# B's queries and scores ahead of A's in a hybrid-attention layer, with query and key copies made on chip

## The chip, the cores and the metric

The kernel runs on one core of a Trainium2 chip. The metric is the device time of one execution in microseconds (us), the median of several runs on the same chip.

## The reference

Two decoder layers run for a prompt of 1024 tokens and 32 sample tokens (8 sequences of 4). Layer 0 is the one that the change touches:

```python
qa, ka, va, qb, kb, vb, z = split(x @ w_in)       # rotary on qa, ka, qb, kb
oa = banded_attention(qa, ka, va, 128, sinks)     # A: 8 query heads, 2 key heads of 64
for g, (window, dil) in enumerate([(128, 1), (512, 4), (2048, 16)]):
    obs[g], lses[g] = banded_attention(to_sub(qb[g], dil), to_sub(kb[g], dil),
                                       to_sub(vb[g], dil), window // dil)
ob = sum(softmax(lses)[g] * obs[g])               # B: three dilated groups, merged
mix = concat([oa, ob]) * silu(z)
x = layer_norm(ALPHA * x + mix @ w_out)
```

The sample tokens do the same against caches. Layer 1 is an mLSTM (chunkwise matrix memory) with its own projections and out-projection. All of it is in float32.

## The kernel before

Every product of float32 matrices is made from pairs of fp32r tiles: a high part (rounded copy, `hi`, on ScalarE) and a low part (the difference, `lo`, on VectorE), three matmuls for one (L199 to L201 for projections, tile `pj`).

Layer 0 first projects keys and values (`proj_kv`, to about 110 us). Then 24 feature tiles of 128 columns follow, 72 matmuls each: 16 for the queries (`proj_q(g)`, g = 0 is A, g = 1, 2, 3 are B with dilation 1, 4, 16, four tiles each), 8 for the gates (`proj_z0(j)`; for j < 4 it also loads A's finished output, `ao`, and its reciprocal denominators, `aF`, and multiplies them in). Queries go as high and low rows to a DRAM tensor `QQ[g]` and are read back by head.

Attention runs by group g, key head kv (0 or 1) and quarter hf of the tokens. First a statistics pass: scores `st` from the high parts alone (L437, queries in `QZ`), their masked row maximum on VectorE (L441, `ST`), transposed (`trm`) and written negated (`NM`) into row 128 of QQ. For B the three groups share one maximum: each group's row goes through `NMB` and `nr` (`attn_b_max`). Then come the scores `sc`: L466 multiplies K1 (high keys twice) with Q1 (low and high queries), L467 K2 (low keys and a row of ones) with Q2 (high queries and the row of negative maxima). ScalarE takes the exponential (L469), GpSimd masks it (L472 to L480), `hi` and `lo` split it (`ph`, `pl`; every fourth `pl` of B on GpSimd), and three matmuls `av` (L489 to L491) multiply it with V. A block is 2 `sc` and 3 `av`. VectorE adds `av` into `OD` (L535, L582, L584). At a half's end `OD` is stored to DRAM, and `finish` loads the denominators back (`dn`), inverts them and stores them (`FD`). All these DMAs are issued by SP, whose queue runs in order: a wait at one holds those behind it.

`weave` takes steps of several generators in proportion to given weights, which sets the order in which code is written; attention is written with a higher scheduling priority (`ahead`), and a scheduler then decides the order on each engine. The first weave puts A's attention and the statistics of B's groups 1 and 2 next to `proj_q(1..3)`; the second puts the statistics of group 3, B's attention for kv = 0 and 9 steps of kv = 1 next to the gates. What is left of kv = 1 runs with the sample attention (`sS`, `so`, tiles `KT`) and the merges, and the out-projection (`py`, weights `wo` split into `oh` and `ol`) follows.

Of the kernel before, what the change touches and what calls it, by code (L numbers as in the profile page):

```python
# [61 lines left out]

AHEAD = (1000, 1000, 60, 300)

W1, W2, W3, W4 = (129, 76), (86, 80), (28, 15, 6), (64, 90)

EARLY = 9

# [29 lines left out]
class Builder:  # L98
# [118 lines left out]
    def proj_q(self, g):  # L217
        nc = self.nc
        dil = DIL[g]
        QQ = self.QQ[g]  # L220
        for j in range(4):
            sh = self.stage.tile([128, T], F32R, tag="sh", name="sh")
            sl = self.stage.tile([128, T], F32R, tag="sl", name="sl")
            qs = self.stage.tile([128, TS], F32, tag="qs", name="qs")

            def evac(c, t0, n, ps):
                src = ps
                if j == 3:
# [12 lines left out]

                s = src[:, :n]
                if dil > 1:
                    s = s.rearrange("p (n r) -> p n r", r=dil)
                self.hi(pv(sh), s, 0.125)
                self.lo(pv(sl), s, pv(sh), 0.125)

            yield from self.proj_feat(self.A['w0f'][4 + 4 * g + j], self.X0, evac)
            r0 = 128 * ((j + 1) % 4)
            self.store('q', QQ[512 + r0:640 + r0, :], f(sh[:, :TP]))  # L250
            self.store('q', QQ[r0:r0 + 128, :], f(sl[:, :TP]))
            self.store('q', self.QS[g, r0:r0 + 128, :], qs)

    def proj_kv(self):
        nc, A, O = self.nc, self.A, self.O
        tc = self.tc
        with tc.tile_pool(name="kvp", bufs=1) as kp, tc.tile_pool(name="kvt", bufs=2) as kt:
# [36 lines left out]
            for j in range(4):  # L294
                sh = self.stage.tile([128, T], F32R, tag="sh", name="sh")
                sl = self.stage.tile([128, T], F32R, tag="sl", name="sl")
                self.hi(sh[:, :TP], KF[:, j, :TP])
                self.lo(sl[:, :TP], KF[:, j, :TP], sh[:, :TP])
                r0 = 128 * ((j + 1) % 4)
                for u in range(2):  # L300
                    self.store('k', self.KK[512 * u + r0:512 * u + r0 + 128, :], f(sh[:, :TP]))
                self.store('k', self.KK[1024 + r0:1152 + r0, :], f(sl[:, :TP]))
                self.store('k', self.KS[r0:r0 + 128, :], KF[:, j, TP:T])
            wv = []
            for k in range(0, 8, 2):
# [51 lines left out]
    def qh_load(self, g, kv, hf):  # L357

        Q = self.QZ[hf % 2]
        t = slice(256 * hf, 256 * hf + 256)  # L360
        h = slice(4 * kv, 4 * kv + 4)
        self.store("Qh", f(Q[0:64]), self.QQ[g].rearrange("(d h) t -> d h t", h=8)[64:128, h, t])
        return Q

    def q2_load(self, g, kv, hf):
        Q2 = self.qp.tile([65, 4, 256], F32R, tag="Q2", name="Q2")
        t = slice(256 * hf, 256 * hf + 256)
        h = slice(4 * kv, 4 * kv + 4)
        self.load(f(Q2), self.QQ[g].rearrange("(d h) t -> d h t", h=8)[64:129, h, t])
        return Q2  # L370

    def k1_load(self, g, kv):
        nc = self.nc
        dil = DIL[g]
        src = self.KK.rearrange("(d h) t -> h d t", h=8)[2 * g + kv][0:128]
        K1 = self.kp.tile([128, TP], F32R, tag="K1", name="K1")
        if dil == 1:
            self.load(f(K1), src)
        else:
            kt = self.kp.tile([128, TP], F32, tag="kt", name="kt", bufs=1)  # L380
            self.load(kt, src)
            nc.vector.tensor_copy(K1.rearrange("p (r n) -> p n r", r=dil), kt.rearrange("p (n r) -> p n r", r=dil))
        return K1

    def k2_load(self, g, kv):
        nc = self.nc
        dil = DIL[g]
        src = self.KK.rearrange("(d h) t -> h d t", h=8)[2 * g + kv][128:192]
        K2 = self.kp.tile([65, TP], F32R, tag="K2", name="K2")
        if dil == 1:  # L390
            self.load(f(K2[0:64]), src)
        else:
            kt = self.kp.tile([128, TP], F32, tag="kt", name="kt", bufs=1)
            self.load(kt[0:64], src)
            nc.vector.tensor_copy(K2[0:64].rearrange("p (r n) -> p n r", r=dil),
                                  kt[0:64].rearrange("p (n r) -> p n r", r=dil))
        nc.gpsimd.memset(f(K2[64:65]), 1.0)
        return K2

    def v_load(self, g, kv):  # L400

# [119 lines left out]

    def attn_a(self, kv):
        nc = self.nc
        K1, K2, V = self.k1_load(0, kv), self.k2_load(0, kv), self.v_load(0, kv)
        ST = self.sm.tile([128, 32], F32, tag="ST", name="ST")
        for hf in range(4):
            Q1 = self.qh_load(0, kv, hf)
            yield from self.stats(0, kv, hf, Q1, K1, ST)
        nc.vector.tensor_tensor(ST, ST, self.sinkb[:, 32 * kv:32 * kv + 32], OP.max)
        nm = self.QQ[0][1024 + 4 * kv:1028 + 4 * kv]  # L530
        self.neg_rows(ST, nm)
        OD = self.odp.tile([65, 4, TP], F32, tag="OD", name="OD")

        def emit(qb, av):
            nc.vector.tensor_copy(self.od_view(OD, 0, qb), self.av_view(av[0:65], 0))  # L535

        for hf in range(4):
            Q1 = self.q1_load(0, kv, hf)
            Q2 = self.q2_load(0, kv, hf)
            yield from self.scores(0, kv, hf, Q1, Q2, K1, K2, V, emit)  # L540
        self.store('o', self.OD[0][kv], OD)
        self.finish(0, kv, nm)

    def attn_b_stats(self, g, kv):
        K1 = self.k1_load(g, kv)
# [24 lines left out]
    def attn_b(self, kv, done=None):  # L570
# [1 line left out]
        nc = self.nc  # L572
        OD = self.odp.tile([65, 4, TP], F32, tag="OD", name="OD")
        for g in (3, 2, 1):
            K1, K2, V = self.k1_load(g, kv), self.k2_load(g, kv), self.v_load(g, kv)

            def emit(qb, av, g=g):
                o = self.od_view(OD, g, qb)
                a = self.av_view(av[0:65], g)
                if g == 3:  # L580
                    for s in range(2):
                        nc.vector.tensor_copy(o[:, :, s, :], a[:, :, s, :])  # L582
                else:
                    nc.vector.tensor_tensor(o, a, o, OP.add)  # L584
                if g == 1 and qb in (2, 5, 7):
                    t = slice(CH[qb // 3][0], 128 * qb + 128)
                    self.store('o', self.OD[1][kv][:, :, t], OD[:, :, t])
                    if done:
                        done(qb // 3)

            for hf in range(4):
                Q1 = self.q1_load(g, kv, hf)
                Q2 = self.q2_load(g, kv, hf)
# [295 lines left out]
    def layer0(self):  # L889
# [4 lines left out]
        self.QQ = [dt(f"QQ{g}", [129 * 8, TP]) for g in range(4)]  # L894
        self.QS = dt("QS", [4, 512, TS])

        self.KK, self.KS = dt("KK", [3 * 512, TP]), dt("KSd", [512, TS])
# [16 lines left out]
        with tc.tile_pool(name="qp", bufs=2) as self.qp, tc.tile_pool(name="kp", bufs=2) as self.kp, \  # L914
# [9 lines left out]
            self.QZ = [sm.tile([128, 4, 256], F32R, name=f"QZ{u}") for u in range(2)]  # L924
            for Q in self.QZ:
                nc.gpsimd.memset(f(Q[64:128]), 0.0)
            run(self.proj_q(0))
            self.done = 0
            self.bps = AB_PS[0]

            def projections():
# [1 line left out]
                    yield from self.proj_q(g)  # L933
                    self.done = g

            def attention():
                for kv in range(2):
                    yield from self.attn_a(kv)
                for g in (1, 2):
                    while self.done < g:  # L940
                        yield None
                    for kv in range(2):
                        yield from self.attn_b_stats(g, kv)

            weave((projections(), W1[0]), (ahead(tc, attention(), AHEAD[0]), W1[1]))

            tmp.release()
            tmp = self.tmp = tc.alloc_tile_pool(name="tmpz", bufs=1, side="right")

            def gate_path():  # L950
                for j in range(8):
                    yield from self.proj_z0(j)

            def last(c):
# [3 lines left out]
            def attention_b():  # L958
# [2 lines left out]
                    self.attn_b_max(kv)  # L961
                self.bps = AB_PS[1]
                yield from self.attn_b(0)
                late = self.late = self.attn_b(1, last)
                for _ in range(EARLY):
                    yield next(late)

            weave((gate_path(), W2[0]), (ahead(tc, attention_b(), AHEAD[1]), W2[1]))
            tmp.release()
# [653 lines left out]
```

## Time and profile before

| | |
|---|---|
| median of 3 runs | 1516.51 us (1511.09 to 1520.24) |
| profiled execution | 1514.5 us, span 1512.8 us |
| mean granted TensorE clock | 0.971 of full speed |
| PE / VectorE / ScalarE / GpSimd busy | 93% / 59% / 31% / 18% |
| bytes moved by DMA queues | 241.01 MB |

The span runs from the first to the last instruction. PE is TensorE's matmuls, SPq SyncE's issue queue. Line numbers are those of the kernel before.

### The profile page before, as it was taken

How to read it: one execution, taken by the hardware profiler on the slowest of the kernel's cores; microseconds unless marked ns; L12 is line 12 of the kernel's file. 1: busy time of each engine (PE TensorE's matmuls, PEld its weight loads, DVE VectorE, ACT ScalarE, POOL GpSimd, SP SyncE). 2: the span in 40 equal slices, each digit the busy share in tenths (PEclk: the TensorE clock that was granted, in tenths of full speed). 3: DMA queues.
4: the chain of work that ended last, by engine and by line, in shares of the span. 5: the costliest groups of instructions: out<-in, count | busy, mean ns of one | idle time of the engine just before them, and what ended most of it. 6: DMA issues, size and time to landing. Idle time of an engine off the chain costs nothing.

```text
span 1512.8 us, 21927 instructions
## 1 busy us (share of the span) xinstructions
PE 1409.6 (93%) x7792; PEld 1193.2 (79%) x7792; DVE 897.7 (59%) x2479; ACT 472.9 (31%) x892; POOL 276.4 (18%) x351
## 2 busy tenths in 40 slices
PE   8999999999988777978999999999999999999997
PEld 7989998998887434456879878988898899877785
DVE  5311556677655856758774536555565566566786
ACT  5331143521112654512124313331333133323310
POOL 1002252512334874401000000000000000000010
PEclk9999999999999978989999999999999999999999
DMA  8646665667747998894312565364224312341731
GB/s 304 222 150 209 212 187 184 188 199 202 205 135 183 226 228 179 260 273 137 128 51 72 193 222 178 97 217 135 70 78 124 116 49 68 118 127 28 239 133 46
DMA packets 149323, 241.01 MB, mean 159 GB/s; under 512 B 17632, under 2 KB 115904, under 8 KB 148696
## 3 DMA queue, kind: packets, MB, share of 16 engines
q1 hardware_dynamic: 141150, 218.24, 49.0%
q10 hardware_dynamic: 8064, 21.37, 3.9%
q8 instruction: 62, 1.02, 0.3%
q14 instruction: 47, 0.39, 0.1%
HBM read 178.66 MB, written 83.97 MB: 174 GB/s over the span
## 4 chain that ended last, share of the span: by engine, by line
PE 67%; DMA 18%; DVE 7%; issue 3%; ACT 1%; POOL 1%; SPq 1%; DVEq 0%; POOLq 0%; ACTq 0%
PE pj L199 10%; PE pj L200 10%; PE pj L201 10%; PE py L167 3%; PE py L165 3%; PE py L166 3%; PE pvo L165 3%; PE pvo L166 3%; PE pvo L167 3%; DMA G<-GR 2%; DMA Q<-QQ 2%; DMA NMB<-NM 1%; DMA QZ<-QQ 1%; DMA OD<-OD 1%; PE av L489 1%
## 5 line engine op out<-in xcount | busy, mean ns | idle before, releaser
L199 PE MATMUL pj<-x1h,wh 128*128 128x384 f32 (+1 forms) x576 | 189.7, 329 | 1.7 <-ACT QT L1156 1.6
L199 PE MATMUL pj<-xh,wh 128*128 128x384 f32 (+1 forms) x576 | 187.9, 326 | 1.2 <-DVE rt L214 1.2
L201 PE MATMUL pj<-x1h,wl 128*128 128x384 f32 (+1 forms) x576 | 187.8, 326 | 0.0
L201 PE MATMUL pj<-xh,wl 128*128 128x384 f32 (+1 forms) x576 | 187.6, 326 | 0.0
L200 PE MATMUL pj<-xl,wh 128*128 128x384 f32 (+1 forms) x576 | 187.6, 326 | 0.0
L200 PE MATMUL pj<-x1l,wh 128*128 128x384 f32 (+1 forms) x576 | 187.6, 326 | 0.0
L199 PEld LDWEIGHTS pj<-x1h,wh 128*128 128x128 f32 x576 | 108.7, 189 | 6.5 <-issue 3.3
L201 PEld LDWEIGHTS pj<-x1h,wl 128*128 128x128 f32 x576 | 108.6, 188 | 6.0 <-issue 5.8
L199 PEld LDWEIGHTS pj<-xh,wh 128*128 128x128 f32 x576 | 109.8, 191 | 4.4 <-DVE rt L214 2.2
L200 PEld LDWEIGHTS pj<-x1l,wh 128*128 128x128 f32 x576 | 108.6, 189 | 4.0 <-issue 3.8
L201 PEld LDWEIGHTS pj<-xh,wl 128*128 128x128 f32 x576 | 110.0, 191 | 1.4
L200 PEld LDWEIGHTS pj<-xl,wh 128*128 128x128 f32 x576 | 109.6, 190 | 1.1
L441 DVE CUSTOM_DVE_ANT_0 junk<-st,maskq 128x256 f32<-128x256 f32 (+1 forms) x256 | 93.0, 363 | 25.0 <-PE st L437 5.9
L165 PE MATMUL pvo<-voh,x1h 128*128 128x512 f32 x256 | 101.7, 400 | 2.5 <-DVE SZ L1172 2.5
L166 PE MATMUL pvo<-voh,x1l 128*128 128x512 f32 x256 | 100.8, 396 | 0.0
L167 PE MATMUL pvo<-vol,x1h 128*128 128x512 f32 x256 | 100.3, 395 | 0.0
L811 POOL TENSOR_TENSOR rsw<-rsw,mhalf 128x1 f32<-128x1 f32 (+1 forms) x54 | 40.2, 745 | 321.4 <-DVE rsw L810 305.6
L122 POOL TENSOR_TENSOR wl<-wr,wh 128x1024 fp32r<-128x1024 f32 x24 | 59.2, 2470 | 122.5 <-ACT qs L233 77.8
L116 DVE TENSOR_TENSOR pl<-p,ph 128x512 fp32r<-128x512 f32 x82 | 68.3, 842 | 21.7 <-ACT ph L112 15.8
L112 ACT ACTIVATE wh<-wr 128x1024 fp32r<-128x1024 f32 x48 | 50.7, 1057 | 81.5 <-PE pj L200 75.2
L112 ACT ACTIVATE ph<-p 128x512 fp32r<-128x512 f32 x100 | 61.4, 629 | 41.6 <-PE av L490 26.2
L469 ACT ACTIVATE p<-sc 128x512 f32<-128x512 f32 x100 | 56.8, 593 | 44.6 <-PE sc L467 29.1
(349 smaller groups left out, 3145.3 us busy)
## 6 DMA issues: line engine op xcount, KB each, us to landing
Q<-QQ SPq DMA_DIRECT2D x32, 512.0 KB
out_kvs_dram<-in_cache_b_kv_dram SPq DMA_DIRECT2D x16, 1022.0 KB
wr<-in_w0f_dram SPq DMA_DIRECT2D x24, 512.0 KB
wr<-in_w1f_dram SPq DMA_DIRECT2D x24, 512.0 KB
Q<-QQ SPq DMA_DIRECT2D x32, 260.0 KB
QQ<-sh ACTq DMA_DIRECT2D x16, 512.0 KB
QQ<-sl ACTq DMA_DIRECT2D x16, 512.0 KB
QZ<-QQ SPq DMA_DIRECT2D x32, 256.0 KB
```

The costliest lines, as they stand in the source:

```text
L112: return self.nc.scalar.activation(out, in_, AF.Copy, scale=scale)
L116: return self.nc.vector.tensor_tensor(out, in_, f(hi), OP.subtract)
L122: self.nc.gpsimd.tensor_tensor(out, in_, f(hi), OP.subtract)
L165: nc.tensor.matmul(ps, xh[:, k, t], wh, start=k == 0, stop=False)
L166: nc.tensor.matmul(ps, xl[:, k, t], wh, start=False, stop=False)
L167: nc.tensor.matmul(ps, xh[:, k, t], wl, start=False, stop=k == 7)
L199: nc.tensor.matmul(ps[:, :n], wh[:, k, :], xh[:, k, :n], start=k == 0, stop=False)
L200: nc.tensor.matmul(ps[:, :n], wh[:, k, :], xl[:, k, :n], start=False, stop=False)
L201: nc.tensor.matmul(ps[:, :n], wl[:, k, :], xh[:, k, :n], start=False, stop=k == 7)
L441: nc.vector.tensor_tensor_reduce(junk[:, :n], st[:, u, c0:c0 + n], mk, 1.0, -3e38, OP.add, OP.max, ST[:, 8 * h + qb:8 * h + qb + 1])
L469: nc.scalar.activation(p, sc, AF.Exp)
L811: nc.gpsimd.tensor_tensor(r, v, self.mhalf[:m], OP.pow)
```

## The change

Three edits. First, the order: A's queries are projected after B's, at the head of the second weave; A's attention moves out of the first weave into the second, behind B's attention for kv = 0; the gates come in the order 4, 5, 6, 7, 0, 1, 2, 3, and those with j < 4 wait, while code is written, until A's half is `attended`. Second, the high query rows of Q2 are copied on ScalarE from Q1, and only row 128 is loaded; QQ's high and low rows change places for it. Third, keys are stored once less, K1's second half is copied on ScalarE, and one load of 128 rows serves K1 and K2.

```diff
-W1, W2, W3, W4 = (129, 76), (86, 80), (28, 15, 6), (64, 90)
+W1, W2, W3, W4 = (129, 15), (129, 96), (28, 15, 6), (64, 90)
...
-            self.store('q', QQ[512 + r0:640 + r0, :], f(sh[:, :TP]))
-            self.store('q', QQ[r0:r0 + 128, :], f(sl[:, :TP]))
+            self.store('q', QQ[r0:r0 + 128, :], f(sh[:, :TP]))
+            self.store('q', QQ[512 + r0:640 + r0, :], f(sl[:, :TP]))
...
-                for u in range(2):
-                    self.store('k', self.KK[512 * u + r0:512 * u + r0 + 128, :], f(sh[:, :TP]))
-                self.store('k', self.KK[1024 + r0:1152 + r0, :], f(sl[:, :TP]))
+                self.store('k', self.KK[r0:r0 + 128, :], f(sh[:, :TP]))
+                self.store('k', self.KK[512 + r0:640 + r0, :], f(sl[:, :TP]))
...
-        self.load(f(Q2), self.QQ[g].rearrange("(d h) t -> d h t", h=8)[64:129, h, t])
+        self.load(f(Q2[64:65]), self.QQ[g].rearrange("(d h) t -> d h t", h=8)[128:129, h, t])
+        self.nc.scalar.activation(Q2[0:64], f(Q1[0:64]), AF.Copy)
         return Q2
...
+    def k_load(self, g, kv, low=True):
...
+            n = 128 if low else 64
             kt = self.kp.tile([128, TP], F32, tag="kt", name="kt", bufs=1)
+            self.load(kt[:n], src[:n])
+            for u, d in enumerate((K1[0:64], K2[0:64]) if low else (K1[0:64],)):
+                nc.vector.tensor_copy(d.rearrange("p (r n) -> p n r", r=dil),
+                                      kt[64 * u:64 * u + 64].rearrange("p (n r) -> p n r", r=dil))
+        nc.scalar.activation(K1[64:128], f(K1[0:64]), AF.Copy)
...
-            run(self.proj_q(0))
-            self.done = 0
+            self.done = self.attended = 0
...
-            def attention():
-                for kv in range(2):
-                    yield from self.attn_a(kv)
+            def statistics():
...
-            weave((projections(), W1[0]), (ahead(tc, attention(), AHEAD[0]), W1[1]))
+            weave((projections(), W1[0]), (ahead(tc, statistics(), AHEAD[0]), W1[1]))
...
             def gate_path():
-                for j in range(8):
+
+                yield from self.proj_q(0)
+                self.done = 4
...
+                for j in (4, 5, 6, 7, 0, 1, 2, 3):
+                    while j < 4 and self.attended <= j // 2:
+                        yield None
                     yield from self.proj_z0(j)
...
                 yield from self.attn_b(0)
+                self.bps = AB_PS[0]
+                while self.done < 4:
+                    yield None
+                for kv in range(2):
+                    yield from self.attn_a(kv)
+                    self.attended = kv + 1
+                self.bps = AB_PS[1]
```

**Where rows move.** TensorE's order where A passes from key head 0 to 1. Before, the transposition `trm` of the second half's maxima stands among projections:

```order
L200 MATMUL pj<-xl_103,wh 128x384
L201 MATMUL pj<-xh_102,wl 128x384
L199 MATMUL pj<-xh_104,wh 128x288
L466 MATMUL sc<-Q_2261,K_2056 128x512
L200 MATMUL pj<-xl_105,wh 128x288
L449 MATMUL trm<-ident,ST 32x128
L201 MATMUL pj<-xh_104,wl 128x288
L199 MATMUL pj<-xh_104,wh 128x288
```

After, at the same place (`st` are the statistics, the numbers mark tiles):

```order
L485 MATMUL av<-ph,V 66x512
L486 MATMUL av<-ph,V 64x512
L487 MATMUL av<-pl,V 66x512
L433 MATMUL st<-K_4718,QZ_951 128x256 x4
L433 MATMUL st<-K_4718,QZ_950 128x256 x8
L433 MATMUL st<-K_4718,QZ_951 128x256 x8
L462 MATMUL sc<-Q_4925,K_4718 128x512 x2
L445 MATMUL trm<-ident,ST 32x128
L463 MATMUL sc<-Q_4927,K_4719 128x512 x2
L462 MATMUL sc<-Q_4925,K_4718 128x512
L463 MATMUL sc<-Q_4927,K_4719 128x512
```

No projection row stands in the 78 rows around this place (the last one ahead of them is followed by 13 blocks of A); the next comes eight rows further on.

SyncE's DMA order at the same hand-over (OD_89 is A's output of key head 0, QQ_75 A's queries). Before:

```order
L109 DMA OD_89<-OD 65x4096
L109 DMA QZ_954<-QQ_76 64x4x256
L109 DMA wr<-in_w0f_dram 128x1024
L109 DMA dn<-OD_89 32x128
L109 DMA QZ_955<-QQ_76 64x4x256
L109 DMA QQ_75<-NM 32x128
L109 DMA FD_93<-dn 32x128
L106 DMA Q_2263<-QQ_75 65x4x256
```

And after:

```order
L109 DMA OD_89<-OD 65x4096
L106 DMA V<-VV 64x8x128
L109 DMA dn<-OD_89 32x128
L109 DMA ao<-OD_89 64x1024 x2
L109 DMA FD_93<-dn 32x128
L109 DMA aF<-FD_93 64x512 x4
L109 DMA QQ_75<-NM 32x128
L106 DMA Q_4927<-QQ_75 1x4x256
```

The row of maxima has moved behind FD and four `aF` loads, and Q2's load shrinks from 65 rows to one. TensorE's order at the end of layer 0's attention, before:

```order
L491 MATMUL av<-pl,V 66x512
L727 MATMUL so<-scrh,scrl 128x128
L165 MATMUL py<-oh,mh_5699 128x512
L166 MATMUL py<-oh,ml_5700 128x512
L165 MATMUL py<-oh,mh_5699 128x512
L166 MATMUL py<-oh,ml_5700 128x512
L165 MATMUL py<-oh,mh_5699 128x512
L166 MATMUL py<-oh,ml_5700 128x512
L732 MATMUL so<-KT,scrh 32x128 x16
```

After:

```order
L681 MATMUL sS<-KT,scrh 32x128 x8
L650 MATMUL sNew<-scrh 128x32 x4
L650 MATMUL sNew<-scrh,scrl 128x32 x4
L487 MATMUL av<-pl,V 66x512
L165 MATMUL py<-oh,mh_5725 128x512
L166 MATMUL py<-oh,ml_5726 128x512
L165 MATMUL py<-oh,mh_5725 128x512
L166 MATMUL py<-oh,ml_5726 128x512
```

Before, all sample scores `sS` stand ahead of the last `av`; after, the first eight do, and the rest with every `pT` and `so` stands behind it.

## Rows read from the trace of the kernel before

**Rows 1.** The page's head and its part 1: busy time, share, instructions.

```profile
span 1512.8 us, 21927 instructions
PE 1409.6 (93%) x7792; PEld 1193.2 (79%) x7792; DVE 897.7 (59%) x2479; ACT 472.9 (31%) x892; POOL 276.4 (18%) x351
```

**Rows 2.** Windows by stage: length, engines' busy time, granted clock, DMA share, GB/s.

```profile
110.00:320.00 210.00, 207.00 (x1233) 194.97 (x1232) 108.59 (x283) 73.88 (x134) 72.58 (x59) 0.99 0.61 191
320.00:497.00 177.00, 155.69 (x929) 146.50 (x927) 116.53 (x420) 33.36 (x62) 54.35 (x49) 0.96 0.68 191
497.00:641.00 144.00, 113.27 (x449) 59.31 (x448) 101.00 (x165) 79.66 (x155) 87.86 (x104) 0.86 0.92 224
641.00:697.00 56.00, 40.07 (x248) 28.41 (x248) 35.44 (x41) 12.86 (x16) 1.82 (x1) 0.88 0.81 237
697.00:785.00 88.00, 87.75 (x432) 70.30 (x431) 68.67 (x156) 13.19 (x25) 9.67 (x11) 1.00 0.32 104
```

**Rows 3.** Windows of 20 to 60 us inside those stages, same columns.

```profile
120.00:140.00 20.00, 20.00 (x127) 20.00 (x126) 2.66 (x5) 3.39 (x7) 6.62 (x4) 1.00 0.55 192
200.00:220.00 20.00, 20.00 (x112) 17.98 (x112) 14.70 (x22) 12.02 (x22) 12.95 (x12) 1.00 0.68 192
440.00:500.00 60.00, 49.13 (x259) 42.16 (x258) 36.49 (x99) 15.59 (x30) 22.39 (x30) 0.94 0.62 166
500.00:540.00 40.00, 31.62 (x116) 18.15 (x114) 35.92 (x47) 27.76 (x49) 38.18 (x35) 0.91 1.05 241
540.00:580.00 40.00, 25.24 (x64) 13.32 (x65) 17.37 (x29) 15.28 (x28) 19.88 (x37) 0.70 0.92 189
```

**Rows 4.** One window, instructions of projection tile pj alone (PE, PEld, DVE, ACT).

```profile
200.00:220.00 20.00, 14.42 (x81) 13.40 (x81) 3.92 (x8) 0.86 (x1) 1.00 0.68 192
```

**Rows 5.** The stage 497 to 641, tile sc alone, then av alone.

```profile
497.00:641.00 144.00, 42.04 (x114) 22.79 (x114) 35.21 (x61) 0.86 0.92 224
497.00:641.00 144.00, 65.80 (x199) 28.75 (x198) 40.84 (x58) 0.86 0.92 224
```

**Rows 6.** SyncE's timeline: start, length of issue, instruction.

```profile
262.55 0.32 SPq L109 DMA_DIRECT2D QQ<-NM  x1
...
263.96 0.78 SPq L106 DMA_DIRECT2D Q<-QQ  x2
...
318.41 0.53 SPq L109 DMA_DIRECT2D OD<-OD  x1
...
328.14 0.32 SPq L109 DMA_DIRECT2D dn<-OD  x1
...
336.32 0.32 SPq L109 DMA_DIRECT2D FD<-dn  x1
...
370.38 1.09 SPq L109 DMA_DIRECT2D aF<-FD  x2
...
375.70 1.08 SPq L109 DMA_DIRECT2D aF<-FD  x2
...
562.91 0.33 SPq L109 DMA_DIRECT2D dn<-OD  x1
...
576.66 0.32 SPq L109 DMA_DIRECT2D FD<-dn  x1
```

**Rows 7.** The page's part 6, DMA issues of Q2: count, KB each.

```profile
Q<-QQ SPq DMA_DIRECT2D x32, 260.0 KB
```

**Rows 8.** The page's part 5, groups: busy, mean ns of one, idle before.

```profile
L112 ACT ACTIVATE wh<-wr 128x1024 fp32r<-128x1024 f32 x48 | 50.7, 1057 | 81.5 <-PE pj L200 75.2
L469 ACT ACTIVATE p<-sc 128x512 f32<-128x512 f32 x100 | 56.8, 593 | 44.6 <-PE sc L467 29.1
```

**Rows 9.** PE's waits from 497 to 641: us in total, times, longest.

```profile
PE sc L467 <- DMA Q<-QQ: 7.4, 7, 3.4
PE sc L466 <- DMA Q<-QQ: 6.6, 4, 2.9
```

**Rows 10.** The stage 697 to 785, out-projection tile py alone.

```profile
697.00:785.00 88.00, 73.89 (x311) 55.10 (x309) 10.71 (x16) 1.00 0.32 104
```

More of the change, by code (lines that the diff above doesn't have):

```diff
@@ L361, in qh_load, with q2_load @@
         h = slice(4 * kv, 4 * kv + 4)
-        self.store("Qh", f(Q[0:64]), self.QQ[g].rearrange("(d h) t -> d h t", h=8)[64:128, h, t])
+        self.store("Qh", f(Q[0:64]), self.QQ[g].rearrange("(d h) t -> d h t", h=8)[0:64, h, t])
         return Q
-    def q2_load(self, g, kv, hf):
+    def q2_load(self, g, kv, hf, Q1):
         Q2 = self.qp.tile([65, 4, 256], F32R, tag="Q2", name="Q2")
@@ L368, in q2_load @@
         h = slice(4 * kv, 4 * kv + 4)
-        self.load(f(Q2), self.QQ[g].rearrange("(d h) t -> d h t", h=8)[64:129, h, t])
+        self.load(f(Q2[64:65]), self.QQ[g].rearrange("(d h) t -> d h t", h=8)[128:129, h, t])
+        self.nc.scalar.activation(Q2[0:64], f(Q1[0:64]), AF.Copy)
         return Q2
-    def k1_load(self, g, kv):
+    def k_load(self, g, kv, low=True):
         nc = self.nc
         dil = DIL[g]
-        src = self.KK.rearrange("(d h) t -> h d t", h=8)[2 * g + kv][0:128]
+        src = self.KK.rearrange("(d h) t -> h d t", h=8)[2 * g + kv]
         K1 = self.kp.tile([128, TP], F32R, tag="K1", name="K1")
+        K2 = self.kp.tile([65, TP], F32R, tag="K2", name="K2") if low else None
         if dil == 1:
-            self.load(f(K1), src)
+            self.load(f(K1[0:64]), src[0:64])
+            if low:
+                self.load(f(K2[0:64]), src[64:128])
         else:
+            n = 128 if low else 64
             kt = self.kp.tile([128, TP], F32, tag="kt", name="kt", bufs=1)
[L381 to L398, printed above, removed]
+            self.load(kt[:n], src[:n])
[3 more added lines that the diff above has]
+        nc.scalar.activation(K1[64:128], f(K1[0:64]), AF.Copy)
+        if low:
+            nc.gpsimd.memset(f(K2[64:65]), 1.0)
+        return K1, K2
     def v_load(self, g, kv):
@@ L523, in attn_a @@
         nc = self.nc
-        K1, K2, V = self.k1_load(0, kv), self.k2_load(0, kv), self.v_load(0, kv)
+        (K1, K2), V = self.k_load(0, kv), self.v_load(0, kv)
         ST = self.sm.tile([128, 32], F32, tag="ST", name="ST")
@@ L538, in attn_a @@
             Q1 = self.q1_load(0, kv, hf)
-            Q2 = self.q2_load(0, kv, hf)
+            Q2 = self.q2_load(0, kv, hf, Q1)
             yield from self.scores(0, kv, hf, Q1, Q2, K1, K2, V, emit)
@@ L544, in attn_b_stats @@
     def attn_b_stats(self, g, kv):
-        K1 = self.k1_load(g, kv)
+        K1 = self.k_load(g, kv, False)[0]
         ST = self.sm.tile([128, 32], F32, tag="ST", name="ST")
@@ L574, in attn_b @@
         for g in (3, 2, 1):
-            K1, K2, V = self.k1_load(g, kv), self.k2_load(g, kv), self.v_load(g, kv)
+            (K1, K2), V = self.k_load(g, kv), self.v_load(g, kv)
             def emit(qb, av, g=g):
@@ L592, in attn_b @@
                 Q1 = self.q1_load(g, kv, hf)
-                Q2 = self.q2_load(g, kv, hf)
+                Q2 = self.q2_load(g, kv, hf, Q1)
                 yield from self.scores(g, kv, hf, Q1, Q2, K1, K2, V, emit)
@@ L895, in layer0 @@
         self.QS = dt("QS", [4, 512, TS])
-        self.KK, self.KS = dt("KK", [3 * 512, TP]), dt("KSd", [512, TS])
+        self.KK, self.KS = dt("KK", [2 * 512, TP]), dt("KSd", [512, TS])
         self.VV = dt("VV", [TP, 8 * 128])
@@ L943, in attention @@
                         yield from self.attn_b_stats(g, kv)
-            weave((projections(), W1[0]), (ahead(tc, attention(), AHEAD[0]), W1[1]))
-            tmp.release()
-            tmp = self.tmp = tc.alloc_tile_pool(name="tmpz", bufs=1, side="right")
+            weave((projections(), W1[0]), (ahead(tc, statistics(), AHEAD[0]), W1[1]))
             def gate_path():
-                for j in range(8):
+                yield from self.proj_q(0)
+                self.done = 4
+                self.tmp.release()
+                self.tmp = tc.alloc_tile_pool(name="tmpz", bufs=1, side="right")
+                for j in (4, 5, 6, 7, 0, 1, 2, 3):
+                    while j < 4 and self.attended <= j // 2:
+                        yield None
                     yield from self.proj_z0(j)
@@ L968, in layer0 @@
             weave((gate_path(), W2[0]), (ahead(tc, attention_b(), AHEAD[1]), W2[1]))
-            tmp.release()
+            self.tmp.release()
             stage.release()
```

## The prediction

> **What bounds the kernel now.** I read the page's totals first, then the table by stage, then finer windows, then who waits for whom. TensorE (PE) is busy 1409.6 of 1512.8 us [rows 1], so time can come only from stretches where it is not full, or runs slowly. The table by stage [rows 2] shows them. From 110 to 320 us PE is busy 207.0 of 210; from 320 to 497, the end of layer 0's last projection, 155.7 of 177. From 497 to 641, B's attention with no projection left to put between its matmuls, 113.3 of 144 at a mean granted clock of 0.86. From 641 to 697 the sample attention ends and the out-projection waits for its weights and merged inputs: 40.1 of 56. From 697 to 785 the out-projection runs full. Everything behind 785 us is layer 1, which the diff does not touch. So I price three stretches: W, the 24 feature tiles (110 to 497, 387 us); U, attention without cover (144 us); T, sample and out-projection (56 + 88 = 144 us).
>
> An attention matmul has two prices. Covered: 127 projection matmuls fill 20 us, 0.157 each [rows 3]; in 200 to 220 us 112 ran without a gap, 81 of them projections [rows 3, 4], so the other 31 took 20 - 81 x 0.157 = 7.3 us, 0.23 each. Uncovered: 116 in 40 us from 500 to 540, 0.34 each, with VectorE busy 35.9 and GpSimd 38.2 of those 40 [rows 3]: the softmax engines and the loads set the pace there. A lower bound is PE's own busy time in that window, 31.6 / 116 = 0.27.
>
> **Part 1: work moved from U into W.** U holds 114 score (sc) and 199 output (av) records [rows 5]. In the order of before, 114 sc and 204 av rows stand behind the last projection; in the order after, 70 and 123, and W holds 125 more sc and av than before. Nearly all of the sample attention has left U as well: it stands behind the last av now. W pays 125 x 0.23 = **+29 us** (bounds 125 x 0.16 = 20, as if they cost what a projection does, and 125 x 0.34 = 43). U keeps 193 matmuls: 193 x 0.34 = 66 us (bounds 52 by 0.27, 66). To it comes the end of A's second half: finish() stores OD, loads dn, divides and stores FD through SP's queue, and VectorE's queue stops at dn. Before, the same end of B's first half fell into 540 to 580 us, where PE was busy 25.2 of 40 at a clock of 0.70 [rows 3], 15 us lost; with half the query bytes in the queues I take 6 (bounds 0 and 15). So U is 72 us in place of 144: **-72 us** (52 to 81).
>
> **Part 2: a new gap at A's hand-over.** Gates j < 4 are written out only once A's half is attended, so the projections run out: the order shows A's last blocks of half 0, all statistics of half 1, and the first scores of half 1 without a projection row between. About 13 blocks of 5 matmuls lose their cover; A has no GpSimd subtraction, so I charge 4 of the 65 x (0.34 - 0.23) = 7 us: **+4 us** (0 to 7). Then PE's queue holds L463's score, which needs Q2's row of negative maxima. On SP the store QQ<-NM now stands behind dn, two ao, FD and four aF; before, directly behind dn and ahead of FD. The links, from the trace: OD store to dn load 318.41 to 328.14, 9.7 us; dn to FD 8.2; FD's landing before aF may issue, taken as a 16 KB store to the next load that needs it, 262.55 to 263.96, 1.4; the second aF pair behind GpSimd's product of the first, 370.38 to 375.70, 5.3; its issues 1.1; QQ<-NM 1.4; the 4 KB row itself at most another 1.4 or so [rows 6]. That is 28.5 us. PE has 20 statistics (5 us at 0.23) and some 6 av (2 us at 0.34) in it: 21.5, **+22 us**. Bounds: if aF's wait vanishes, 22 - 5.3 = 16; with the dn to FD of the crowded 562.91 to 576.66, 13.75 [rows 6], 27. Queued behind that score are the gates' projections, so nothing fills it. The Trainium skill ("DMA: Bandwidth & Descriptors", Anatomy of one DMA) puts the fixed cost of a DMA at about 2.0 us and says that DMA engines do not wait on semaphores, the issuing sequencer does. By its cost six small links and 2.4 us of data would be 14 us, 20 with 6 of engine work, and the gap some 13, the net -14, 1500 us; the rows show 9.7 for the first link alone, and I keep the rows. Its second sentence is what the order of SP's rows makes visible: everything behind aF waits with it.
>
> **Part 3: chains that gain cover.** From 440 to 500 us, where the last B statistics, the common maximum and B's first loads follow each other, PE is busy 49.1 of 60 [rows 3]. After, the same chain has A's queries and gates 4 to 7 beside it, and I take back nearly all of the 10.9: **-10 us** (0 to -11). A's own statistics lie in such cover too, as before.
>
> **Part 4: copies in place of loads.** 32 Q2 loads of 260 KB become rows of 4 KB [rows 7], 8.2 MB; four K stores of 512 KB go, 2 MB; keys' loads lose about 3.6 MB. In exchange ScalarE makes 46 copies of 1024 elements, at 1.06 us [rows 8] 49 us on an engine that is busy 31% [rows 1]. In W it is free; in U some 12 copies come to exponentials (0.59 each [rows 8]) and splits. PE waited for Q 14.0 us in U [rows 9], which is in the 0.34 price; since the copies take back what the loads give, I leave that price. In W the queues' share is 0.61 to 0.68 [rows 2], so fewer bytes change little: **0**; what it may be worth is in the relief below.
>
> **Part 5: the tail T grows.** The sample's 16 large key and value loads now stand on SP behind the last query, between merges and weights, and 336 of the 432 out-projection matmuls behind the sample. Counted from the order behind OD's last store: 21.3 MB against 12.5. At T's 237 GB/s [rows 2] the 8.8 MB more are 37 us if transfers are the bound; the queues' share was 0.81 [rows 2], so 0 if all falls into their gaps and PE's. I take 15. Then 336 matmuls at 88 us / 311 [rows 10] are 95 for 88: +7. **+22 us** (7 to 44).
>
> **Sum.** -72 + 29 + 4 + 22 - 10 + 22 = -5. From the profiled execution's 1514.5 us this is 1509.5; the median of the runs shown is 1516.5, 0.1% above it, and I say **1509 us**. No change and 0.5% (7.6 us) can't be told apart here.
>
> **Rivals.**
> *The tail decides (slower).* At a tail of +40, near its upper bound, the net is +13: 1527 us. It decides as soon as the tail costs more than 27, where the net turns positive. For it: the sample's buffers are four deep, and SP waited for sS, which frees them, in U; a slow round in T has no attention beside it. Against it: PE is idle for 16 of those 56 us already [rows 2].
> *Copies block exponentials (slower).* ScalarE takes its queue in order; a Q2 copy at the head waits for Q1's load, and the exponentials of blocks already scored wait behind it. At 1.4 us [rows 6] for each of the 12 in U, net +12: 1527 us; it decides from 0.4 us each. Against it: two query buffers are loaded ahead.
> *The relief is worth more (faster).* If U runs at PE's own 0.27 with no gap (52 us, 20 less), and the tail costs only its 7 (15 less), net -40: 1474 us. For it: the queues' share is 1.05 from 500 to 540 [rows 3], and PE's largest waits in U are for Q [rows 9]. Against: VectorE and GpSimd are as full there.
> *Only moved (no change).* The matmuls are the same ones; if W and T give back what U saves, the time stays. In the sum 29 + 4 + 22 - 10 + 22 = 67 of the 72 do so already, so this lies inside the forecast's own spread.
>
> **How the numbers follow.** Forecast as summed, 1495 to 1523: 0.45 (0.21 faster, 0.19 same, 0.05 slower). Tail: 0.25 (0.06 same, 0.19 slower). Copies: 0.08, slower. Relief: 0.22, faster. Together faster 0.43, same 0.25, slower 0.32. The range must reach the relief's 1474 and the slower rivals' 1527, and some of each side's spread; 1473 to 1535 leaves about 2 in 10 out: the better half of the relief, both slower rivals at once, or a gap at the hand-over twice as long.
>
> **What would show it.** Right: about 70 us between the last projection and the last av; one PE gap of about 22 us some 60 us ahead of the last projection, which ends with a load of 4 KB behind QQ<-NM; out-projection starting in earnest about 70 us after the last av; layer 1 as long as before. Wrong: projections inside the hand-over, so that no gap shows; waits of exponentials for Q2's copies; or a U of over 85 us.

## The result and the profile after

The change made the kernel slower, by 1 to 1.5%: 1534.43 us median (1530.03 to 1537.07) against 1517.68 before, ratio 1.0114 (95% interval 1.0073 to 1.0156). A second measurement gave 1532.50 against 1512.06, ratio 1.0148 (1.0123 to 1.0174). The forecast was 1509, 0.5% faster.

The windows of the changed kernel, by stage, columns as in [rows 2]. The cuts are those of after: 341 is about the end of the first weave, 478 to 526 the hand-over inside A, 551 the last projection of layer 0, 634 the last av, 709 the last sample matmul, 798 the last of the out-projection.

```profile
110.00:320.00 210.00, 198.12 (x1238) 194.36 (x1237) 110.97 (x406) 53.26 (x88) 45.88 (x27) 0.98 0.56 177
320.00:341.00 21.00, 17.95 (x104) 17.15 (x103) 17.84 (x62) 3.06 (x4) 6.48 (x4) 0.93 0.39 127
341.00:478.00 137.00, 132.09 (x723) 115.20 (x722) 84.19 (x175) 79.36 (x134) 65.36 (x81) 1.00 0.51 153
478.00:526.00 48.00, 25.84 (x83) 14.78 (x82) 28.14 (x84) 16.06 (x29) 11.82 (x14) 0.68 0.45 129
526.00:551.00 25.00, 24.88 (x139) 21.31 (x138) 13.11 (x20) 14.42 (x25) 11.91 (x13) 1.00 0.30 94
551.00:634.00 83.00, 62.04 (x227) 35.51 (x225) 53.12 (x76) 54.29 (x88) 61.99 (x72) 0.84 0.60 175
634.00:709.00 75.00, 56.45 (x339) 34.98 (x338) 49.13 (x78) 21.38 (x42) 3.66 (x2) 0.76 0.96 295
709.00:798.00 89.00, 82.92 (x386) 65.71 (x382) 65.77 (x146) 11.96 (x22) 9.13 (x10) 0.94 0.33 112
```

The reader is to see three things. U, without cover, fell from about 146 us to 83. W grew from 385 to 441 (110 to 551): its one deep hole is the hand-over, PE busy 25.8 of 48 at a clock of 0.68, and it has also lost 9 us of PE between 110 and 320, where [rows 2] were full. T grew: 164 us from the last av to the last out-projection matmul, where 134.7 were needed before. The table has the last starts from the traces (projection, av, out-projection, us) and what follows from them:

| | last pj | last av | last py | W | U | T |
|---|---|---|---|---|---|---|
| before | 494.7 | 640.2 | 774.9 | | 145.5 | 134.7 |
| after | 550.9 | 633.8 | 797.9 | +56 | -63 | +29 |

Layer 1 took as long as before (736 us from the last py to the end, against 738). So the +23 us at the end of layer 0 are the whole loss.

The sample's first key loads tell where T starts. The loads of `KT` by SyncE, before and then after (median issue time, first and last start):

```profile
L106 SPq DMA_DIRECT2D KT<-in_kt_dram x12: 328/336/424, 578.2 to 617.3; - x12
```

```profile
L106 SPq DMA_DIRECT2D KT<-in_kt_dram x12: 328/368/839, 618.0 to 669.8; - x12
```

Before, the first came 62 us ahead of the last av; after, 16 us. The sample then ended 75 us behind the last av, where it had ended 21 us behind.

The hand-over, in the timelines of after, SyncE, then TensorE, then VectorE, then ScalarE (start, length, instruction, idle time and what ended it):

```profile
495.12 0.57 SPq L109 DMA_DIRECT2D OD<-OD  x1
...
503.60 0.33 SPq L109 DMA_DIRECT2D dn<-OD  x1
...
506.92 0.31 SPq L109 DMA_DIRECT2D FD<-dn  x1
508.86 6.02 SPq L109 DMA_DIRECT2D aF<-FD  x4
514.97 0.53 SPq L109 DMA_DIRECT2D QQ<-NM  x1
517.68 1.26 SPq L106 DMA_DIRECT2D Q<-QQ  x2
```

```profile
501.07 0.79 PE L433 MATMUL st<-K,QZ 128*128 128x256 f32 x2 [0.25 <-DVE ST L437]
507.23 0.79 PE L433 MATMUL st<-K,QZ 128*128 128x256 f32 x2 [5.37 <-DVE ST L437]
...
512.35 0.41 PE L445 MATMUL trm<-ident,ST 128*32 128x128 f32 x1
519.59 1.22 PE L463 MATMUL sc<-Q,K 65*128 65x512 f32 x2 [6.82 <-DMA Q<-QQ]
```

```profile
505.40 0.28 DVE L514 TENSOR_TENSOR dn<-dn,nmc 32x128 f32<-32x128 f32 x1 [4.39 <-DMA dn<-OD]
```

```profile
512.80 0.27 ACT L447 ACTIVATE NM<-trm 32x128 fp32r<-32x128 f32 x1 [22.44 <-PE trm L445]
```

The maxima were there only at 513.1 us. SyncE issued their store at 514.97, so the four aF loads ahead of it cost 2 us. What came late was the maxima themselves: VectorE stood 4.4 us at dn with statistics behind it in its queue, and PE waited 5.4 us there.

### The profile page after: what moved, and what is told of

It reads as the page before. It is cut to its first block, busy times and chain, and to the rows that moved or that the text cites. A ratio compares the mean times of both kernels' runs of the same rounds, so it can differ in the third digit from the quotient of the medians.

```text
span 1534.1 us, 22001 instructions
## 1 busy us (share of the span) xinstructions
PE 1414.5 (92%) x7792; PEld 1200.1 (78%) x7792; DVE 897.3 (58%) x2480; ACT 515.4 (34%) x938; POOL 266.6 (17%) x350
## 4 chain that ended last, share of the span: by engine, by line
PE 69%; DMA 16%; DVE 7%; issue 3%; ACT 2%; POOL 1%; SPq 1%; ACTq 0%; DVEq 0%; POOLq 0%
PE pj L199 11%; PE pj L200 10%; PE pj L201 10%; PE py L165 3%; PE py L167 3%; PE py L166 3%; PE pvo L165 3%; PE pvo L166 3%; PE pvo L167 3%; DMA wr<-in_wo_dram 3%; DMA G<-GR 2%; PE st L433 2%; DMA out_cmems_dram<-Cs 1%; DMA aF<-FD 1%; PE sc L462 1%
## 5 line engine op out<-in xcount | busy, mean ns | idle before, releaser
L116 DVE TENSOR_TENSOR pl<-p,ph 128x512 fp32r<-128x512 f32 x83 | 64.7, 794 | 42.9 <-ACT ph L112 42.1
L165 PE MATMUL py<-oh,mh 128*128 128x512 f32 x128 | 55.3, 432 | 16.0 <-ACT oh L112 10.4
L433 PE MATMUL st<-K,QZ 128*128 128x256 f32 x256 | 52.3, 299 | 18.5 <-DVE ST L437 9.6
```

The lines of the kernel that those rows point to most:

```text
L116: return self.nc.vector.tensor_tensor(out, in_, f(hi), OP.subtract)
L165: nc.tensor.matmul(ps, xh[:, k, t], wh, start=k == 0, stop=False)
L433: nc.tensor.matmul(st[:, u, :], Q1[:, h, q0:q0 + 128], K1[:, w0:w0 + 256], start=True, stop=True)
```

## The experiments

Times are medians; the ratio, with its 95% interval, is to before, measured beside it on the same chip. Where two runs of different rounds are subtracted, the medians are from different chips; by the ratios such differences come out within about 3 us of those given. W, U and T are read from the traces as above, KT is the first load of the sample's keys.

### The two halves of the change

e1 takes the copies and leaves the order of before; e2 the other way round (the diff is the one at the top, cut in two).

> The order of before, with only the copies in place of loads (QQ's rows swapped, Q2 and K1 copied on ScalarE, 14 MB fewer). If the copies are harmless, as the prediction charged them, the time is that of before within 8 us, a few us less if PE's 14 us of waits for Q in the uncovered stretch shrink: 1508 to 1518. If they block exponentials at the head of ScalarE's queue, 10 or more us above before, 1527 and up, and they carry the loss.

> The order of after, with before's loads of Q2 and keys. If the order carries the loss, this stands 15 to 30 us above before (1532 to 1547), as far as after or further, since the 14 MB come back. If the copies carry it, it falls to before or below, 1505 to 1520.

e1: 1500.40 us, 0.9930 (0.9904 to 0.9956), faster. e2: 1539.22, 1.0175 (1.0137 to 1.0212), slower. They about add up to the change: -11 and +27 make 16, where it measured 17 and 20. The order carries the loss. The copies gained more than either theory had it: U fell from 145.5 to 138.3 us and T from 134.7 to 124.8. In e1's stretch without cover, 492 to 630 us, PE's waits for Q, where [rows 9] had 14.0 us, and for ScalarE are these (us, times, longest):

```profile
PE av L485 <- ACT ph L112: 6.7, 6, 4.2
...
PE sc L462 <- DMA Q<-QQ: 3.5, 2, 2.8
...
PE sc L462 <- ACT p L465: 2.2, 3, 1.2
...
PE sc L463 <- ACT Q L370: 0.3, 1, 0.3
```

The wait for the copy itself is 0.3 us. All of PE's waits for ScalarE's copies, exponentials and high parts here are 9.2 us, against 5.9 before, so ScalarE's extra work took back some 3 us of the 10 that the loads gave.

### The hand-over

e3 puts A's row of maxima and Q2's row on ScalarE's queue; e4 takes dn off VectorE; e6 makes the closing of A's first half wait for the second half's row.

```diff
-        self.neg_rows(ST, nm)
+        self.neg_rows(ST, nm, 'q')            # e3: ScalarE's queue; Q2's row of A too
...
-        nc.vector.reciprocal(dn, dn)
...
+            nc.gpsimd.tensor_tensor(dn, dn, e, OP.pow)      # e4: e is -0.5
+            nc.gpsimd.tensor_tensor(dn, dn, dn, OP.mult)
...
+                for _ in range(9):
+                    yield next(second)
+                self.finish(0, 0, self.QQ[0][1024:1032])    # e6: reads both halves' rows
```

> After, with the store of A's row of maxima and Q2's row loads for A on ScalarE's queue instead of SP's, so that four aF loads no longer stand ahead of them. The prediction's chain (SP's order sets the gap at A's hand-over) expects the gap to close by 7 us or more: 1527 or less. The rival from the trace of after is that VectorE sets it: the maxima are written by ScalarE only at 513.1 us and the store is issued at 514.97, so SP's order costs 2 us at most: 1531 to 1535, no change that can be told.

> After, with A's denominators inverted on GpSimd (power -0.5, squared), so that VectorE's queue no longer stops at dn among the second half's statistics; by the order printed the row of maxima then also stands ahead of FD and aF on SP. If VectorE's stop sets the gap, PE gets its scores 5 to 8 us earlier: 1525 to 1530. If neither matters, because other waits take over, 1532 to 1536.

> After, with the closing of A's first half made dependent on the second half's row of maxima (its load of the row covers both halves), so that by the printed order dn stands behind all statistics on VectorE, and FD and aF behind the row on SP. Theory: the stop at dn (5.4 us) and SP's order (2 to 4 us) are 8 to 11 us of the gap, and PE's L463 comes at about 509 in place of 519.6: 1521 to 1527. Rival: gates 0 and 1 are late by as much as the gap shrinks, since their inputs move back: 1530 to 1535.

e3: 1530.84, 1.0130 (1.0106 to 1.0155), not told from after; L463 came at 518.64 in place of 519.59, although the store of OD was issued 0.9 us later than in after. SyncE's order, which the prediction held for the cause, is worth a few us at most. e4: 1550.86, 1.0263 (1.0240 to 1.0287), 16 to 18 us worse than after, which neither theory had, and yet L463 came at 508.31. The power on GpSimd took 20.7 us, with A's masks queued behind it:

```profile
502.58 20.74 POOL L517 TENSOR_TENSOR dn<-dn,mhalf 32x128 f32<-32x128 f32 x1
```

e6 does it without that price: 1524.23, 1.0099 (1.0066 to 1.0132), 8 us below the second measurement of after, and PE's row reads

```profile
508.04 1.22 PE L463 MATMUL sc<-Q,K 65*128 65x512 f32 x2 [4.16 <-DMA Q<-QQ]
```

That is 11.5 us sooner, of which 3.4 lie ahead of the hand-over (the store of OD is issued at 491.73 in place of 495.12). So some 8 us of the hole are VectorE's stop at dn with the little of SyncE behind it. The gain shows in U, 67 us in place of 83, and not in W, 446 in place of 441: more of the attention now runs ahead of the last projection. The rest of the hole, statistics at VectorE's pace with no projection beside them, stayed.

### The first weave

e7 writes the statistics of B's groups 1 and 2 behind the first weave, at the head of the second.

```diff
-            weave((projections(), W1[0]), (ahead(tc, statistics(), AHEAD[0]), W1[1]))
+            run(projections())
...
             def attention_b():
+                yield from statistics()
```

> After, with the statistics of B's groups 1 and 2 moved from the first weave to the head of the second. After lost 12 us of PE from 110 to 320 us (198.1 busy against 207.0 before, and 0.98 clock). If it is the statistics alone in the stream that stall PE there (VectorE late, QZ loads), the first weave now runs full and, if they are harmless later, the time falls by 5 to 12: 1522 to 1530. If the stalls only move with them, 1532 to 1540.

1531.79, 1.0140 (1.0109 to 1.0172): no change that can be told. But the statistics did not move on the chip. They are written with the higher priority of attention, and the scheduler, probably for that, put them back where they had stood: the first starts at 169.0 us, in after at 170.0. The windows of tile `st` alone, after and then e7 (PE, PEld, VectorE):

```profile
110.00:320.00 210.00, 32.81 (x168) 28.28 (x168) 59.19 (x164) 0.98 0.56 177
```

```profile
110.00:320.00 210.00, 34.16 (x176) 29.57 (x176) 60.57 (x169) 0.99 0.55 179
```

So e7 says nothing on whether the statistics stall the first weave. What PE waited for there is in the trace of after, from 110 to 341 us (us, times, longest):

```profile
PE st L433 <- DMA QZ<-QQ: 6.6, 2, 4.1
PE pj L199 <- DVE rt L214: 3.9, 4, 2.8
PE pj L199 <- DVE sl L117: 3.4, 4, 1.1
PE st L433 <- issue: 1.1, 1, 1.1
```

Before, the same stretch has 4.2 us of waits for QZ and 0.2 for rt. So some 7 us of the loss stand at projections that wait for VectorE (rotary products and low parts), which has twice the statistics to do there (168 `st` matmuls in place of 84). No run separates this.

### The tail

e5 leaves A's product out of gates 2 and 3, whose inputs come last; e12 is the same omission in before; f4 the same in e1; f3 is e5 and e6 together.

```diff
-        if j < 4:
+        if j < 2:
```

> After, with A's output and denominators left out of gates 2 and 3 (no ao, aF, product: part of the result is missing). In after the last aF is issued at 610.6 us, 60 us behind the last gate projection, and the sample's first KT load only at 618.0. If the sample waits for the memory of these gates, KT starts some 30 to 50 us earlier, the sample ends closer behind the last av, and the time falls by 12 to 25 us: 1509 to 1522. If the loads and PE themselves set the tail (the prediction's 8.8 MB), it falls by 5 at most, what the missing loads and SP's waits are worth: 1528 to 1534.

> The control of the run that left A's product out of gates 2 and 3: the same omission in the kernel before, where the last aF is issued at 417.0 us, far ahead of the sample. If the 30 us that it was worth in after came from the sample's memory, here it is worth what the loads and products cost themselves: 1506 to 1512, 0 to 6 us. If the omission itself is worth 15 us or more (1497 or less), the memory explains only the rest.

e5: 1501.85, 0.9940 (0.9916 to 0.9963), 31 us below after, more than the theory's 12 to 25. That looked like the answer, but e12: 1492.69, 0.9897 (0.9881 to 0.9914), 16 us for the omission in before, where the last aF is issued at 417 us, far ahead of the sample. The expectation of 0 to 6 was wrong, and half of e5's gain may be the omission's own. Before has some 13 us of waits for split weights in T, and e12 has 1; why the omission brings those in time was not tested. Hence the pair with a control on one chip:

> After itself once more, on the chip of the three runs below, so that their differences are not taken across chips: 1525 to 1535, 13 to 22 us above before.

> After with both losses taken out at once: A's product left out of gates 2 and 3, and the closing of A's first half behind the second half's row. If they add up (omission alone 1501.9, the row 7 to 10 us): 1491 to 1496. If the gap only covers for a later wait: 1499 to 1504.

> The control for the run above: before's order with the copies and the same omission. The copies were worth 11 us, the omission in before 16; added: 1482 to 1488. If both shorten the same tail and do not add, 1489 to 1496. What the run above stands over this one is what the order still costs once both of its named losses are gone: 3 to 12 us if moving blocks from U to W is itself no gain.

| | | us | ratio (interval) |
|---|---|---|---|
| f1 | after | 1532.50 | 1.0148 (1.0123 to 1.0174) |
| f3 | after, omission and row | 1487.86 | 0.9856 (0.9829 to 0.9883) |
| f4 | before's order with copies, omission | 1493.60 | 0.9892 (0.9859 to 0.9924) |

With the copies the omission is worth some 7 us (1500.4 to 1493.6; the two intervals overlap). In after's order it is worth 31 (e5), and 36 with the row mended (1524.2 to 1487.9). Against this control the products of gates that stand last cost the order 24 to 29 us, give or take some 6; against the 16 us of e12 it would be 15 to 20. The control with the copies is the nearer one, since after has them too. And f3 is no slower than f4: without the late products and the stop at the hand-over, the order neither costs nor gains anything that can be told. By their traces W is 67 us longer in f3 than in f4, U 71 shorter and T 4 longer.

Does the sample's late start cost that? In after, e2 to e4, e6, e7 and f1 the first KT load is issued 6.5 to 8.0 us behind the last aF; in before, e1, e8 to e10, e12, f3, f4 and g1, 1.4 to 2.7 us behind the last FD (in e5 8.1). In the kernel's text the pools of the gates (`tmp`, with aF) and of the closings (`sm`, with dn) are released just ahead of the sample's buffers, so aF and dn may be the last users of the memory that KT gets. f2 and g2 put a wait into e1's order: gate 7's last write reads B's output after so many steps (`held`), and the gates' memory comes free that much later; g1 is g2's control.

```diff
+        if j == 7:
+            while self.held is None:
+                yield None
+            nc.vector.tensor_scalar(junk := self.tmp.tile([65, 16], F32, tag="hold", name="hold"), self.held, 0.0, None, op0=OP.mult)
+            nc.vector.tensor_tensor(sz[:65, :16], sz[:65, :16], junk, OP.add)
         self.store('z', self.SZ[j], sz)
...
-EARLY = 9
+EARLY = 16                                              # g1, g2
```

> Before's order with the copies (first 1500.4), and one wait put in: gate 7's last write also reads B's output of the second half after its ninth step, so that the gates' memory comes free late while all else stays. KT was issued at 567 there. If the memory of late gates is what lengthens the tail, KT moves behind 585 and the time rises by 5 to 15 us, 1505 to 1515. If the sample's start does not matter, 1497 to 1503.

> Before's order with the copies, and 16 in place of 9 steps of B's second half in the second weave; the control for the run below. KT stays right behind FD, at about 565, and the time within 6 us of the 1500.4: 1495 to 1506.

> The same with gate 7's last write waiting for the sixteenth step of B's second half: the wait of the earlier run, which moved KT by 4 us only and told nothing, made to bind. If the memory of late gates lengthens the tail, KT moves to 585 or later and the time stands 8 to 20 us above the control. If the sample's late start does not matter by itself, within 4 us of the control, and the 24 us of late products in after stay open.

f2: 1497.56, 0.9915 (0.9894 to 0.9937), where it should be if the sample's start did not matter; but KT came only 4 us later, at 571.0, so f2 decides little. Its T is 12 us longer than e1's and its U 10 shorter, with no loss of time: T alone is no measure. g1: 1511.15, 0.9996 (0.9971 to 1.0021); g2: 1520.47, 1.0040 (1.0020 to 1.0060). Here it bound: KT at 566.4, then at 585.6.

```profile
L106 SPq DMA_DIRECT2D KT<-in_kt_dram x12: 327/364/749, 566.4 to 618.7; - x12
```

```profile
L106 SPq DMA_DIRECT2D KT<-in_kt_dram x12: 328/405/2008, 585.6 to 633.2; - x12
```

19 us of late start made T 10.5 us longer (153.6 to 164.1), with U the same (122.4 and 122.3), and the kernel 7 to 9 us slower (9 by the medians, 7 by the ratios). At that rate the 49 us by which KT is later in f1 than in e1 (616 against 567) would be some 20 us, most of the 24 to 29. This is an estimate: it takes the loss to grow in proportion far beyond the 19 us tried, and in an order with less attention beside the sample.

g1 itself missed its expectation by 5 us, and is of use: seven more steps of B written ahead made U 16 us shorter and T 29 us longer than in e1, with KT at the same time (566.4 and 567.0). So a late start is not the only thing that lengthens T: attention that is taken away from beside the sample leaves the sample's work to T.

### A's place, the gates' place

e9 puts A ahead of B's first half again. e8 is e1, and e10 is before, with the gates in the order 4 to 7, 0 to 3. e11 gives B's denominators in e8 memory of their own.

```diff
-                yield from self.attn_b(0)               # e9: moved behind A's loop
...
-                for j in range(8):
+                for j in (4, 5, 6, 7, 0, 1, 2, 3):      # e8, e10
...
+            dn = self.cst.tile([128, 32], F32, name="dnb")    # e11, B only
```

> After, with one part undone: A's attention stands ahead of B's first half in the second weave again, so that A's closing chain, the gates' products and B's scores can overlap. Theory (A last is what costs: the hand-over without cover, and gates 2 and 3 holding the sample's memory): 1485 to 1505, KT again right behind B's closing. Rival (the second weave holds too much attention wherever A stands): 1515 to 1535.

> The order of before with the copies (the first run above, 1500.4), and the gates in the order 4 to 7, 0 to 3, one of the change's edits alone. If the gates' order is harmless: 1497 to 1504. If gates that need A's output, placed last, hold the sample's memory longer, 1506 to 1515.

> Before, with the gates in the order 4 to 7, 0 to 3 and nothing else. If the gates' order and the copies add up (1488 with both, 1500 with the copies alone): 10 to 13 us below before, 1499 to 1503. If the copies are needed for it: 1508 to 1516.

> Before's order, copies and gates 4 to 7 first (1488.3), and B's first half's denominators in memory of their own, 128 rows of 32. In all runs KT's first load follows the last user of the released memory within some 2 us to 7 us; here that was FD at 559.8, KT at 562.4. If memory is what the sample waits for, KT starts by about 500 us and the sample leaves the tail, 10 to 30 us less: 1458 to 1478. If the sample only takes the place of B's attention on PE and the queues, 1483 to 1492.

e9: 1524.68, 1.0082 (1.0049 to 1.0114), in the rival's range, far above the theory's 1485 to 1505, although KT is again right behind B's closing. W went back to before's (last projection 490.4) and U beyond it, to 160 us: undoing this part gives up the shorter U as well, so it does not isolate the loss. e8: 1488.25, 0.9868 (0.9824 to 0.9912); e10: 1490.47, 0.9861 (0.9833 to 0.9888). Both came out below all that was expected of them. The gates' order is worth 21 us without the copies and 9 to 12 with them; beside it the copies add nothing that can be told. Both have T at 125 us, as e1 and e12 have; what all four shorten is the same 10 us of tail, and e8 and e10 gain some 8 us in W and 6 in U beside it; why was not tried. e8 and e10 are faster than both kernels. e11: 1501.17, 0.9932 (0.9910 to 0.9955), a miss in time. For the memory it is the plainest run: B's denominators taken out of it, KT was loaded at 498.5, 64 us sooner, and now 6.1 us behind the next user, the last aF. But the first sS still ran at 562.3 (565.4 in e8), and T was 136.3. Loads alone do not start the sample; what else it waits for there was not tried.

## Why the prediction was wrong

**What the sum missed.** By the traces the change is +56 us in W, -63 in U, +29 in T and -2 in layer 1, +21 in all; the sum had 45, -72, 22 and 0, -5 in all. The miss of 26 is spread: W 11, U 9, T 7. Against e1, which has the copies as after has, f1 is +60, -57 and +39. Two steps carry it.

**The first step that failed is the trade of Part 1**, attention moved from U into W. With Parts 2 and 3 it was to bring 27 us net (-72 + 29 + 4 + 22 - 10); it brought 7 against before, and against e1 it lost 3. In f3 against f4, with the hand-over mended and the late products gone, it is 67 for 71, still about even. The rival "only moved" had this right. In W the idle time grew by 18 us, about the 16 charged (4 + 22 - 10), but PE's busy time by 36 where 29 were charged (362.7 in 110 to 497 before, 398.9 in 110 to 551 after): 0.29 for each of the 125 matmuls in place of 0.23. U's 193 matmuls took 83 us, 0.43 each, with 32 of the sample beside them. PE's waits there, 551 to 634 us, are no longer for Q in the main (us, times, longest):

```profile
PE sc L462 <- ACT p L465: 5.5, 4, 3.2
PE sc L462 <- DMA Q<-QQ: 4.0, 1, 4.0
PE av L487 <- POOL pl L481: 3.5, 1, 3.5
PE av L485 <- DVE OD L578: 2.4, 1, 2.4
```

GpSimd is busy 62.0 of those 83 us, as much as PE. Which of these waits keeps U from shrinking further was not tried.

**The second is Part 5, the tail.** It charged 15 of the 37 us that its bytes would take at T's rate, and 7 for matmuls. T grew by 29 against before and by 39 against e1. The windows of T, from the last av to the last py, of before, after, e1 and f3:

```profile
640.20:774.90 134.70, 118.77 (x627) 90.77 (x623) 97.53 (x177) 24.23 (x36) 10.57 (x11) 0.95 0.53 162
```

```profile
633.80:797.90 164.10, 139.47 (x722) 100.77 (x722) 114.88 (x223) 33.30 (x64) 12.79 (x12) 0.85 0.62 196
```

```profile
630.40:755.20 124.80, 116.14 (x613) 90.49 (x612) 93.59 (x173) 23.41 (x34) 10.43 (x11) 0.93 0.54 166
```

```profile
623.00:752.30 129.30, 118.94 (x651) 90.97 (x649) 99.84 (x187) 27.47 (x50) 12.18 (x11) 0.96 0.57 181
```

Length times rate gives 22, 32, 21 and 23 MB: T of after moved some 10 MB more than before, where 8.8 were counted. So the bytes were not mistaken, but they did not fall into gaps, since the queues were busy 0.96 of the 75 us from 634 to 709. And PE was busy 21 us longer than before, at a clock of 0.85 against 0.95: 48 sS and 176 so matmuls of the sample ran behind the last av, where before had 0 and 136 (by the order printed with the change eight sS stand ahead of it; in the trace 16 do), and the sum has no term for these. How the 29 us divide between the full queues and the sample's matmuls is not shown.

What the prediction did not ask is why the loads stand so late. It read their place on SP from the order and priced their bytes. The two gates that stand last need A's last closing chain (FD at 580.9 us in f1, the last aF at 609.6), and the sample's first load follows that by 7 us. In f3, without these two products, KT came at 564.3, all key loads were issued ahead of the last av (564.3 to 609.9, av at 623.0), and T was 129, 4 us above f4's.

**Part 2, the hand-over**, was right in place and size: 478 to 526 us hold 83 matmuls, 19 us at 0.23, so the hole is 29, where 26 were charged. It was wrong in its cause, so the size is in part luck. SyncE's order is worth 2 us (e3 changed nothing that can be told); VectorE's stop at dn and statistics without cover make the hole (e4's L463, e6). The sentence from the Trainium skill ("DMA: Bandwidth & Descriptors", Anatomy of one DMA) on semaphore waits at the issuing sequencer holds in the row of aF, 6.02 us for four issues that take 0.45 to 0.59 us each; it was only not the wait that ended last. The 2.0 us that the prediction took from that section stand there for DMAs issued by GpSimd; these are SyncE's, and the sum did not use them.

**Part 3, cover for B's chain**, held: 132.1 of 137 us are busy from 341 to 478. What it left out is the first weave, 9 us lost where A's scores had filled it; the waits there are for QZ and for VectorE, and their cause stays open, since e7 did not move the statistics.

**Part 4, copies**, was priced 0 and measured -11.5 us (e1). The loads in U were worth most of their waits, 14.0 us down to 3.8, of which ScalarE took back some 3. This gain hid part of what the order lost. The rival "copies block exponentials" was to cost 12 us net and is no cause of the loss: with the copies e1 is faster. The rival "the tail decides" came true in its sign. Its price of 40 is near the 39 only against e1, whose T the copies had shortened by 10; against before T is +29, past its point of 27, and by that alone the sum would have been +2.

Still open is how the 24 to 29 us of late products divide between the sample's start (some 20, estimated from g1 and g2) and GpSimd's and SyncE's waits around them.

## What to carry to other kernels

When a step is moved later, ask what memory and which tiles it holds until then, and who is to get them next: the cost may come up a whole stage further on, where no line of the diff stands. Moving matmuls under cover is no gain while the work that they leave behind (here the sample's loads) had used them as its own cover; price both places. An experiment that leaves work out needs the same omission in the kernel before: here up to half of a clear gain may have been the omission's own. And where a scheduler sets the order, the trace has to show that an edit moved what it was to move: e7's did not.

## What the hardware showed unexpectedly

A power of 32x128 elements on GpSimd took 20.7 us, where a product of the same shape took 0.82 (e4), with masks of 0.6 to 1.1 us queued behind it.

PE's granted clock fell with the holes, to 0.68 over the hand-over's window and to 0.50, the lower of its two levels (1.2 of 2.4 GHz), from 500 to 520 us, where PE was busy 4.6 of 20 us:

```profile
500.00:520.00 20.00, 4.60 (x10) 2.54 (x11) 7.36 (x28) 1.21 (x2) 2.52 (x2) 0.50 0.29 80
```

So a hole costs more than its idle time: the 33 av, 26 st and 18 sc matmuls and few others of that window took 0.31 us of busy time each (25.84 for 83), where covered ones had 0.23.
